# Seven products for both halves of the first FFN, with kept weight parts and an activation that lives in DRAM

## The chip, the cores and the metric

The kernel runs on one core of one Trainium2 chip. The metric is the device time of one execution in microseconds. Beside the times there is one profiled execution, with the span from its first to its last instruction and a trace of every instruction. The engines are PE (TensorE, matrix products), DVE (VectorE), ACT (ScalarE), POOL (GpSimd) and SP (SyncE, which here only issues transfers). ACT and POOL have queues for transfers as well.

## The reference

A bidirectional encoder of two layers is run on 256 prompt tokens and 1024 sample tokens, of width 1024. All arrays are float32. Both layers end in a SwiGLU FFN with inner width 2816:

```python
def _swiglu(h, w_gate, w_up, w_down):
    return (jax.nn.silu(h @ w_gate) * (h @ w_up)) @ w_down

def _trunk(x, ...):
    for i in range(DEPTH):
        j = i // N_MIXERS
        if i % N_MIXERS == 0:
            x = x + _attention(_rms_norm(x, attn_norm_g[j]), w_qkv[j], q_norm_g[j], k_norm_g[j], w_o[j])
        else:
            x = x + _conformer_conv(_rms_norm(x, conv_norm_g[j]), conv_w_in[j], ...)
        x = x + _swiglu(_rms_norm(x, ffn_norm_g[i]), w_gate[i], w_up[i], w_down[i])
    return _rms_norm(x, final_norm_g)
```

The attention ends in `o @ w_o`. The convolution module is a product to twice the width, a gate, a depthwise convolution of width 31 over the tokens, a LayerNorm, a swish and a product back. `_trunk` is applied to the prompt and to the sample.

## The kernel before

**Arithmetic.** Each float32 operand is split into a high part `h` and a low part `l`. ACT casts the high part and DVE subtracts it (`split`, lines 131 and 132). A product is then three matmuls: `wh*h`, `wh*l`, `wl*h`. The 1280 tokens are kept transposed (channels on the 128 partitions, tokens along the free axis) in two halves of 640, `HA` and `HB`. The convolution shifts the cut to 624 and 656 (`CA`, `CB`). A matmul works on half of a half, 320 columns.

**The usual product.** `mm` (line 594) makes one block of 128 output channels from 8 input tiles with 8 x 3 x 2 = 48 matmuls. `weights` (line 138) loads 512 KB of weights to a `raw` buffer and splits them to an `hl` buffer. There are 4 `raw` and 5 `hl` buffers.

**Seven products.** `two_blocks` (line 717) makes two blocks of 128 output channels for both 320-column parts, as a 2 x 2 by 2 x 2 block product with seven block products in place of eight. Each is 4 input tiles x 3 = 12 matmuls (`product`, line 710), so two blocks take 84 matmuls and not 96. `seven` (line 152) loads the two weight blocks to `raw`, forms the sums of their quarters on DVE (lines 170 to 173) and splits the results: three `hl` tiles `t1`, `t3`, `t2` and a half-sized `t4` (tag `h3`, two buffers). `norm7` and `seven_right` (lines 676 and 692) make the activation's sums and splits. The results of the products go to accumulators `y`, `x`, `z` in PSUM, and from there to two rows with copies on ACT and additions on DVE. `acc` hands out four accumulators in turn, to these and to all other products.

**Which FFN uses what.** In layer 0 the first half uses seven products and the second half the usual ones. In layer 1 it is the other way round: first half usual, second half seven. `ffn` takes the blocks of the inner width in groups. With seven products a group is a pair of blocks: gate, then up, then the `down` product of the group before (lines 848 to 854). `down` (line 833) has two weight tiles for a pair; for each of the 8 output tiles it runs 24 matmuls and adds the result on DVE to the tile of `x` that is resident in SBUF (line 840).

**Slots.** Activations of all kinds share 48 slots of 688 columns (`slot`). Three more buffers, tag `ld`, take tiles that come from DRAM (`loaded`). `x_d` in DRAM holds a copy of `x`, by half.

**Order.** The order on PE is written out by hand, by generators that `drive` (line 1107) interleaves: a main generator, and background generators that advance by so many steps at each of its yields. The order on all other queues is made at build time by a planner, which takes each instruction when by its own estimate its inputs and buffers are ready. What runs on the chip is that fixed order; an instruction that is not ready holds up what is queued behind it on its engine. The sequence of layer 0 (lines 1124 to 1143) is: `heads(HA)` splits the attention's output; `attn_out(HA)`, the product with `w_o`, beside `heads(HB)`; `attn_out(HB)`, all 8 output tiles, beside `norm7(HA)`; `ffn(0)` on HA; one group of `ffn(0)` on HB beside the norm of HA; `conv_in` on HA; the rest of `ffn(0)` on HB. The depthwise convolution of HA (`conv_mid`, line 933, 31 DVE instructions for each of 8 tiles) runs as background beside `conv_in` and the rest of that FFN.

Of the kernel before, what the change touches and what calls it, by code (L numbers as in the profile page):

```python
# [69 lines left out]
def trunk(ctx: ExitStack, tc: tile.TileContext, a: dict):  # L70
# [6 lines left out]
    x_d = dram.tile([D, T], F32, name="x_d")  # L77

# [73 lines left out]
    def seven(src1, src2):  # L152


        q = D // 2
        raws = []
        for src in (src1, src2):
            raw = wp.tile([P, D], F32, tag="raw", bufs=RAW, name="raw")
            nc.sync.dma_start(raw.rearrange("p (k c) -> p k c", k=NK), src)
            raws.append(raw)  # L160
        a, b = raws

        def parts(raw):
            hl = wp.tile([P, 2, D], F32R, tag="hl", bufs=WEIGHTS, name="hl")
            split(hl[:, 0, :], hl[:, 1, :], raw)
            return hl

        t1 = parts(a)
        third = hp.tile([P, q], F32, tag="third", bufs=THIRDS, name="third")
        V.tensor_tensor(out=third, in0=a[:, :q], in1=b[:, :q], op=ALU.subtract)  # L170
        V.tensor_tensor(out=b[:, :q], in0=b[:, :q], in1=b[:, q:], op=ALU.add)
        V.tensor_tensor(out=a[:, :q], in0=b[:, :q], in1=a[:, :q], op=ALU.subtract)
        V.tensor_tensor(out=a[:, q:], in0=a[:, q:], in1=a[:, :q], op=ALU.subtract)
        t3, t2 = parts(a), parts(b)
        t4 = hp.tile([P, 2, q], F32R, tag="h3", bufs=THIRDS, name="h3")
        split(t4[:, 0, :], t4[:, 1, :], third)
# [499 lines left out]
    def norm7(half, row, ops, load, box):  # L676
# [4 lines left out]
        for k in range(NK // 2):  # L681
# [7 lines left out]
            seven_right(f[0][:, :n], f[0][:, n:2 * n], f[1], n, ops)  # L689
            yield  # L690

    def seven_right(b11, b12, low, n, ops):

# [10 lines left out]
        for x, pair in ((low, (2, 3)), (t12, (5, 6)), (t34, (7, 4))):  # L704
            h, l = hl_pair("b")
            split(h[:, :2 * n], l[:, :2 * n], x[:, :2 * n])
            for i, c in zip(pair, (slice(0, n), slice(n, 2 * n))):
                ops[i].append((h[:, c], l[:, c]))
# [8 lines left out]
    def two_blocks(src, f, ops, n, corner):  # L717
# [3 lines left out]
        left = seven(*(src[:, g * P:(g + 1) * P].rearrange("(k p) c -> p k c", p=P) for g in (f, f + 1)))  # L721
# [32 lines left out]
    def attn_out(half, os_, xs, each):  # L754
        for ct in range(NK):
# [25 lines left out]
    def ffn(layer, hn, xs, half, groups, closing=None, each=None):  # L781
# [4 lines left out]
        last = groups[-1][-1]  # L786

# [16 lines left out]
        def up2(f):  # L804
# [3 lines left out]
            g1, g2 = two_blocks(a["w_gate"][layer], f, hn, n, gate_corner)  # L808
# [7 lines left out]
            u1, u2 = two_blocks(a["w_up"][layer], f, hn, n, up_corner)  # L816
# [8 lines left out]
        def ups(fs):  # L825
            if isinstance(hn, dict):
                for f in fs[::2]:
                    yield from up2(f)
            else:
                for f in fs:  # L830
                    yield from up(f)

        def down(fs, seen):
            wd = [weights(a["w_down"][layer, f * P:(f + 1) * P, :].unsqueeze(1)) for f in fs]
            acts = [hs.pop(f) for f in fs]
            for ct in range(NK):
                pd = acc("pd")
                o = slice(ct * P, (ct + 1) * P)
                mm(pd, lambda k: (wd[k][:, 0, o], wd[k][:, 1, o]), acts, n, True, True)
                V.tensor_tensor(out=two(xs[ct], half), in0=pd[:, :, :n], in1=two(xs[ct], half), op=ALU.add)  # L840
# [7 lines left out]
        for fs in groups:  # L848
            early = fs if closing is not None and fs[-1] == last else fs[:2 if isinstance(hn, dict) else 1]
            yield from ups(early)  # L850
            if prev is not None:
                yield from down(prev, len(early) == len(fs) and fs[-1] == last)
            yield from ups(fs[len(early):])
            prev = fs
# [22 lines left out]
    def back(xs, half, row, out, box):  # L877

        for ct in range(NK):
            xs.append(slot("x"))  # L880
            nc.sync.dma_start(xs[ct][:, :half.len], x_d[ct * P:(ct + 1) * P, half.lo:half.hi])
        yield from norm(xs, half, row, out, box)

    def sevens():
        return {i: [] for i in range(1, 8)}
# [237 lines left out]
    with tc.manual_schedule(engines={mybir.EngineType.PE}):  # L1123
        oa, ob, xa, xb, ha, hb = [], [], [], [], sevens(), []
# [4 lines left out]
        tot, take = taken(HB)  # L1129
        drive(attn_out(HB, ob, None, take),  # L1130
              first(factors(tot_a, HA, RMS_EPS, box), norm7(HA, R_F0, ha, lambda ct: xa[ct], box)), 2)
        gs = groups(2, 2, 2, 2, 2, 2, 2, 2, 2, 2, 2)
        drive(ffn(0, ha, xa, HA, gs), back(xb, HB, R_F0, hb, box_b), 3, factors(tot, HB, RMS_EPS, box_b))
        hc, u, c, y, box = [], [], [], [], []
        gs = groups(3, 3, 4, 4, 4, 4)
        drive(ffn(0, hb, xb, HB, gs[:1]), norm(xa, HA, R_CONV, hc), 2)
        spill(xa, HA)
        w = CA.len + GAP
        bg = conv_mid(u, w, c, box)
        drive(conv_in(hc, HA, u), bg, RATE0, finish=False)  # L1140
# [57 lines left out]
```

## Time and profile before

| | |
|---|---|
| median of 3 runs | 2964.31 us (2963.46 to 2966.57) |
| profiled execution, its own time | 2959.4 us |
| its span | 2957.4 us |
| mean granted clock of TensorE | 0.991 |
| transfers, read and written | 220.37 MB and 34.01 MB |
| `ffn(0)` on HA | 752.5 to 1194.9 us |
| `ffn(0)` on HB, first group | 1194.9 to 1265.7 us |
| `conv_in` on HA | 1265.7 to 1378.4 us |
| `ffn(0)` on HB, the rest | 1378.4 to 1783.4 us |

The page gives for each engine the time in which it was busy; the view of windows gives the same for a stretch, with the number of instructions begun in it, the granted clock and the busy share of the 16 DMA engines. The timeline lists instructions in order, and in square brackets how long the engine was idle before one and what ended that wait. The chain of waits follows the work that ended last back to its start. The time of the profiled execution lies 4.9 us below the median of the runs.

### The profile page before, as it was taken

Reading aid. Unit: us, or ns where it says so; the run is one execution under the profiler, and the core shown is the slowest. Engines: PE = TensorE matmul, PEld = TensorE weight load, DVE = VectorE, ACT = ScalarE, POOL = GpSimd, SP = SyncE. Lnnn points to the kernel's source line nnn. Section 1 sums busy time; section 2 is a strip of 40 time slices with the busy share of each in tenths; the row PEclk is TensorE's granted clock in tenths of the full one; section 3 lists DMA queues with packets and bytes.
Section 4 is the critical chain, followed back from the end, with each engine's and each line's share of the span. In section 5 each row is a group of like instructions: output and inputs, shape, how many; then the busy total and the mean of one; then the engine's idle time right before and its main releaser. Section 6 shows DMA issues by size and latency. Waiting matters only on the chain.

```text
span 2957.4 us, 46658 instructions
## 1 busy us (share of the span) xinstructions
PE 2876.9 (97%) x18837; PEld 2755.3 (93%) x18837; DVE 2210.3 (75%) x3501; ACT 1179.5 (40%) x1835; POOL 445.4 (15%) x403
## 2 busy tenths in 40 slices
PE   8989999999999999999999999999999998999997
PEld 6767888789999999999999999999999998999997
DVE  7988999965767677677998446889985438767675
ACT  4438888863433333322212234222222324333332
POOL 2545555421100000100000102000001001000000
PEclk9999999999999999999999999999999999999999
DMA  4532232144222223322222224222223322422221
GB/s 151 180 122 58 55 86 60 44 122 124 91 86 82 76 84 121 116 79 74 67 75 68 83 90 139 72 75 76 68 69 94 96 77 94 137 82 73 84 72 51
DMA packets 323680, 262.65 MB, mean 89 GB/s; under 512 B 18392, under 2 KB 285664, under 8 KB 323464
## 3 DMA queue, kind: packets, MB, share of 16 engines
q1 hardware_dynamic: 309688, 240.26, 27.7%
q10 hardware_dynamic: 12336, 14.16, 1.4%
q0 software_dynamic: 1440, 5.24, 0.6%
q8 instruction: 148, 2.42, 0.3%
q14 instruction: 68, 0.56, 0.1%
HBM read 220.37 MB, written 34.01 MB: 86 GB/s over the span
## 4 chain that ended last, share of the span: by engine, by line
PE 52%; DVE 4%; DMA 2%; issue 0%; ACT 0%; DVEq 0%; ACTq 0%
PE pd L603 14%; PE pu L603 10%; PE pg L603 10%; PE ci L916 8%; PE co L603 4%; DVE hl L132 1%; DMA raw<-in_w_up_dram 1%; DMA raw<-in_w_gate_dram 1%; PE y L713 1%; PE y L715 1%; PE y L714 1%; PE z L714 0%; PE z L713 0%; PE z L715 0%; PE pd L1074 0%
## 5 line engine op out<-in xcount | busy, mean ns | idle before, releaser
L131 ACT CAST hl<-raw 128x1024 fp32r<-128x1024 f32 x372 | 385.0, 1048 | 877.5 <-issue 380.9
L132 DVE TENSOR_TENSOR hl<-raw,hl 128x1024 fp32r<-128x1024 f32 x372 | 462.4, 1251 | 157.9 <-ACT hl L131 157.3
L603 PE MATMUL pd<-hh,hl 128*128 128x320 f32 (+2 forms) x2752 | 522.4, 309 | 3.0 <-DVE x L840 3.0
L603 PEld LDWEIGHTS pd<-hh,hl 128*128 128x128 f32 x2752 | 433.2, 188 | 3.9 <-DVE x L840 3.5
L944 DVE SCALAR_TENSOR_TENSOR c<-u,cols,c 128x640 f32<-128x640 f32 (+1 forms) x480 | 427.6, 899 | 9.7
L603 PE MATMUL pd<-hl 128*128 128x320 f32 (+2 forms) x1376 | 313.8, 309 | 1.4 <-DVE hl L132 1.4
L840 DVE TENSOR_TENSOR x<-pd,x 128x640 f32<-128x640 f32 (+2 forms) x264 | 215.3, 822 | 131.8 <-PE pd L603 131.6
L603 PE MATMUL pu<-hnh,hl 128*128 128x320 f32 (+1 forms) x1408 | 269.1, 308 | 0.0
L603 PE MATMUL pg<-hnh,hl 128*128 128x320 f32 (+1 forms) x1408 | 269.0, 308 | 0.0
L632 POOL TENSOR_TENSOR sq<-sq 128x640 f32<-128x640 f32 (+2 forms) x63 | 118.0, 1873 | 958.1 <-ACT sq L628 956.6
L603 PEld LDWEIGHTS pd<-hl 128*128 128x128 f32 x1376 | 230.2, 188 | 2.0 <-DVE hl L132 2.0
L603 PEld LDWEIGHTS pg<-hnh,hl 128*128 128x128 f32 x1408 | 221.5, 189 | 0.0
L603 PEld LDWEIGHTS pu<-hnh,hl 128*128 128x128 f32 x1408 | 220.8, 188 | 0.3
L473 DVE TENSOR_SCALAR_CACHE_REDUCE s<-s,r_q 128x1024 f32<-128x1024 f32 (+1 forms) x160 | 181.0, 1132 | 23.1 <-PE s L461 16.7
L132 DVE TENSOR_TENSOR pl<-pt,ph 128x512 fp32r<-128x512 f32 x272 | 186.8, 687 | 15.2 <-ACT ph L131 10.5
L916 PE MATMUL ci<-hnh,hl 128*128 128x320 f32 (+2 forms) x1024 | 192.6, 309 | 0.0
L495 POOL TENSOR_SCALAR p<-p,rl 128x1024 f32<-128x1024 f32 (+1 forms) x160 | 158.8, 997 | 169.1 <-DVE rl L492 129.2
L502 PEld LDWEIGHTS pt<-ident,p 128*128 128x128 f32 x1088 | 132.2, 141 | 53.0 <-DVE pl L132 17.1
L131 ACT CAST ph<-pt 128x512 fp32r<-128x512 f32 x272 | 159.6, 590 | 48.1 <-PE pt L502 38.5
L502 PE MATMUL pt<-ident,p 128*128 128x128 f32 x1088 | 166.2, 275 | 7.6 <-DVE pl L132 4.3
L916 PEld LDWEIGHTS ci<-hnh,hl 128*128 128x128 f32 x1024 | 164.5, 188 | 0.0
L484 ACT ACTIVATE p<-s,nm 128x1024 f32<-128x1024 f32 (+1 forms) x160 | 159.4, 999 | 10.7 <-DVE s L473 7.5
(230 smaller groups left out, 6129.0 us busy)
## 6 DMA issues: line engine op xcount, KB each, us to landing
raw<-in_w_gate_dram SPq DMA_DIRECT2D x88, 512.0 KB
raw<-in_w_up_dram SPq DMA_DIRECT2D x88, 512.0 KB
raw<-in_w_down_dram SPq DMA_DIRECT2D x88, 512.0 KB
raw<-in_conv_w_in_dram SPq DMA_DIRECT2D x32, 512.0 KB
raw<-in_w_qkv_dram SPq DMA_DIRECT2D x20, 512.0 KB
q_d<-qs SPq DMA_DIRECT2D x18, 512.0 KB
raw<-in_w_o_dram SPq DMA_DIRECT2D x16, 512.0 KB
q<-q_d SPq DMA_DIRECT2D x16, 512.0 KB
```

The costliest lines, as they stand in the source:

```text
L131: S.copy(out=dst_h, in_=src)
L132: V.tensor_tensor(out=dst_l, in0=src, in1=dst_h.bitcast(F32), op=ALU.subtract)
L473: V.tensor_scalar(out=s[:, c], in0=s[:, c], scalar1=r_q[self.j // 4][b][:, i, head:head + 1], scalar2=None, op0=ALU.mult, op1=ALU.min, acc ...
L484: S.activation(out=p[:, c], in_=s[:, c], func=AF.Exp, bias=nm[:, i:i + 1], scale=-1.0, accum_out=l[:, i:i + 1])
L495: GP.tensor_scalar(out=p[:, c], in0=p[:, c], scalar1=rl[:, i:i + 1], scalar2=1.0, op0=ALU.mult, op1=ALU.mult)
L502: PE.transpose(ps[:, n * P:(n + 1) * P], self.p[n][:, kt * P:(kt + 1) * P], ident)
L603: PE.matmul(ps[:, c, :n], wt, x[:, c * n:(c + 1) * n], start=first and k == 0 and not end and xi == 0, stop=last and k == nk - 1 and end)
L632: GP.tensor_tensor(out=self.tot, in0=self.tot, in1=new, op=ALU.add)
L713: PE.matmul(ps, wh, h, start=first and k == 0, stop=False, skip_group_check=True)
L840: V.tensor_tensor(out=two(xs[ct], half), in0=pd[:, :, :n], in1=two(xs[ct], half), op=ALU.add)
L916: PE.matmul(ps[:, c, :hi - lo], wt, x[:, lo:hi], start=k == 0 and not end and xi == 0, stop=k == NK - 1 and end)
L944: V.scalar_tensor_tensor(out=c[:, :ln], in0=us[ct][:, k:k + ln], scalar=col(ct, R_DW + k), in1=c[:, :ln], op0=ALU.mult, op1=ALU.add)
```

## The change

`ffn(0)` on HB now also uses seven products. The first half's `seven` stores each finished part (`t1`, `t3`, `t2`, `t4`, high and low) to a DRAM tensor `w7_d`, 3.67 MB for each matrix and pair of blocks. The second half's `seven` loads these parts straight to `hl` and `h3` and does no splits and no sums for gate and up.

```diff
+    w7_d = {(m, f): dram.tile([P, 7, D], F32, name=f"w7_{m}_{f}") for m in ("w_gate", "w_up") for f in range(0, FF // P, 2)}
...
+        def parts(raw, at_k):
+            n = 2 if at_k < 6 else 1
...
+            flat = hl.rearrange("p h c -> p (h c)").bitcast(F32)
+            if src1 is None:
+                nc.sync.dma_start(flat, keep.rearrange("p n c -> p (n c)")[:, at_k * D:(at_k + n) * D])
+                return hl
             split(hl[:, 0, :], hl[:, 1, :], raw)
+            if keep is not None:
+                nc.sync.dma_start(keep.rearrange("p n c -> p (n c)")[:, at_k * D:(at_k + n) * D], flat)
             return hl
```

The second half's `x` is no longer resident during its FFN. `down` loads each tile from `x_d` to an `ld` buffer, adds in place and stores it back through POOL's queue; in the last group the sum goes to a slot and stays.

```diff
+                if stored:
+                    old = loaded("old")
+                    nc.sync.dma_start(old[:, :ln], x_d[o, half.lo:half.hi])
+                    if fs[-1] == FF // P - 1:
+                        x = slot("x")
+                        xs.append(x)
+                    else:
+                        x = old
+                else:
+                    x = old = xs[ct]
                 mm(pd, lambda k: (wd[k][:, 0, o], wd[k][:, 1, o]), acts, n, True, True)
-                V.tensor_tensor(out=two(xs[ct], half), in0=pd[:, :, :n], in1=two(xs[ct], half), op=ALU.add)
+                V.tensor_tensor(out=two(x, half), in0=pd[:, :, :n], in1=two(old, half), op=ALU.add)
+                if stored and x is old:
+                    nc.gpsimd.dma_start(x_d[o, half.lo:half.hi], x[:, :ln])
```

With seven products a group's order becomes gate, `down` of the group before, up (for both halves of layer 0 and for the second half of layer 1); in the last group both gate and up still come first.

The product with `w_o` for HB is made in two portions: output tiles 0 to 3 before `ffn(0)` on HA, beside `norm7(HA)`, and tiles 4 to 7 after it, beside the norm of HA. The splits of the attention's output for HB are made again for the second portion, beside the end of `ffn(0)` on HA. All of `ffn(0)` on HB now comes after `conv_in`, beside which `norm7(HB)` runs, with tiles of `x` loaded from DRAM; its last two splits of every group of four are put off until `conv_in` has ended.

```diff
+        drive(attn_out(HB, ob, None, take_b, range(NK // 2)),
+              first(factors(tot_a, HA, RMS_EPS, box), norm7(HA, R_F0, ha, lambda ct: xa[ct], box)), 4)
+        ob = []
+        tot_a, take_a = taken(HA)
+        drive(ffn(0, ha, xa, HA, pairs, None, lambda ct: take_a(ct, xa[ct])), heads(HB, ob), 2, iter(()))
+        hc, u, c, y, box, box_a = [], [], [], [], [], []
+        drive(attn_out(HB, ob, None, take_b, range(NK // 2, NK)),
+              first(factors(tot_a, HA, RMS_EPS, box_a), norm(xa, HA, R_CONV, hc, box_a)), 3)
+        xa, later = [], []
...
+        drive(conv_in(hc, HA, u),
+              both(first(factors(tot_b, HB, RMS_EPS, box_b), norm7(HB, R_F0, hb, stored(HB), box_b, later)), bg, RATE0),
+              1, finish=False)
+        for pair, x in later:
+            cut7(hb, HB.n, pair, x)
+        drive(ffn(0, hb, xb, HB, pairs, load=True, stored=True), conv_norm(c, box, w, CA, y), 3, bg, RATE)
```

More of the change, by code (lines that the diff above doesn't have):

```diff
@@ L674, in norm, with norm7 @@
             yield
-    def norm7(half, row, ops, load, box):
+    def norm7(half, row, ops, load, box, later=None):
         n = half.n
@@ L703, in seven_right @@
         V.tensor_tensor(out=t4, in0=b21, in1=t2, op=ALU.subtract)
[L704 to L708, printed above, removed]
+        cut7(ops, n, (2, 3), low)
+        return ((5, 6), t12), ((7, 4), t34)
     def product(ps, left, right, first):
@@ L715, in product, with two_blocks @@
             PE.matmul(ps, wl, h, start=False, stop=k == len(right) - 1, skip_group_check=True)
[L717 to L721 removed]
+    def two_blocks(layer, name, f, ops, n, corner, load):
+        keep = w7_d[name, f] if layer == 0 else None
+        src = a[name][layer]
+        left = seven(*(None if load else src[:, g * P:(g + 1) * P].rearrange("(k p) c -> p k c", p=P)
+                       for g in (f, f + 1)), keep)
         y, x, zz = (acc(name)[:, 0, :n] for name in "yxz")
@@ L752, in heads, with attn_out @@
             yield
-    def attn_out(half, os_, xs, each):
-        for ct in range(NK):
+    def attn_out(half, os_, xs, each, cts=range(NK)):
+        for ct in cts:
             old = loaded("old")
@@ L825, in ups @@
         def ups(fs):
[L826 to L831, printed above, removed]
+            for f in fs:
+                yield from up(f)
         def down(fs, seen):
@@ L848, in ffn @@
         for fs in groups:
[L849 to L853, printed above, removed]
+            ending = fs[-1] == last
+            if paired:
+                g = up2(fs[0])
+                yield next(g)
+                if ending:
+                    yield from g
+                if prev is not None:
+                    yield from down(prev, ending)
+                yield from g
+            else:
+                early = fs if closing is not None and ending else fs[:1]
+                yield from ups(early)
+                if prev is not None:
+                    yield from down(prev, len(early) == len(fs) and ending)
+                yield from ups(fs[len(early):])
             prev = fs
@@ L875, in taken, with stored, load @@
         return tot, take
[L877 to L882, printed above, removed]
+    def stored(half):
+        def load(ct):
+            x = loaded("xb")
+            nc.sync.dma_start(x[:, :half.len], x_d[ct * P:(ct + 1) * P, half.lo:half.hi])
+            return x
+        return load
     def sevens():
```

72 lines of the change are left out of this document (37 added, 35 removed).

## The prediction, made before the changed kernel was run

> **What bounds the kernel now.** I read the page's busy times first, then the chain of waits, then windows cut at the stages that the change touches.
>
> ```profile
> span 2957.4 us, 46658 instructions
> ...
> PE 2876.9 (97%) x18837; PEld 2755.3 (93%) x18837; DVE 2210.3 (75%) x3501; ACT 1179.5 (40%) x1835; POOL 445.4 (15%) x403
> ```
> ```profile
> 1385.42 7.03 PE pu L603 x48
> ```
> ```profile
> 752.50:1194.90 442.40, 434.33 (x2937) 431.83 (x2937) 318.80 (x429) 171.41 (x248) 10.09 (x6) 0.99 0.30 93
> 1194.90:1265.70 70.80, 67.89 (x466) 67.11 (x466) 42.14 (x57) 20.87 (x27) 6.42 (x6) 0.99 0.27 81
> 1265.70:1378.40 112.70, 112.70 (x772) 112.70 (x771) 82.55 (x96) 24.29 (x32) 8.88 (x22) 1.00 0.29 85
> 1378.40:1783.40 405.00, 405.00 (x2774) 404.68 (x2774) 302.56 (x354) 106.30 (x135) 34.62 (x20) 1.00 0.25 76
> ```
> ```profile
> 1045.00:1085.00 40.00, 40.00 (x274) 39.86 (x273) 29.02 (x40) 14.68 (x22) 0.00 (x0) 1.00 0.27 80
> ...
> 1434.00:1512.00 78.00, 78.00 (x535) 78.00 (x534) 76.31 (x91) 16.45 (x19) 4.80 (x2) 1.00 0.25 76
> ```
>
> The columns of a window are its length, then busy time and count for PE, PE's weight loads, DVE, ACT and POOL, then clock, DMA share and GB/s. PE is the bound: 97% of the span, and on the chain a block of 48 matmuls takes 7.03 us, 146.5 ns each. At that rate the 2937 matmuls of the first half's FFN need 430.3 us of its 442.4, so it loses 12.1. The second half's two stretches hold 3240 matmuls, 474.7 of 475.8 us. So in this half a matmul less is time less, as long as nothing else comes to the front. DVE is the next engine: from 1434 to 1512, beside the convolution, it was busy for 76.31 of 78.00 us, and PE still lost nothing.
>
> What PE loses, it loses at the joints between stages:
>
> ```profile
> 698.20 3.57 PE L656 MATMUL bc<-ident,rs_r 80*128 80x80 f32 x16 [3.54 <-DVE rs_r L126]
> ...
> 757.35 0.41 PE L714 MATMUL x<-bl,hl 128*128 128x320 f32 x1 [1.48 <-DVE bl L132]
> ...
> 760.75 0.64 PE L713 MATMUL y<-bh,hl 128*128 128x320 f32 x1 [2.83 <-ACT r L726]
> ```
> ```profile
> 1192.30 0.56 PE L603 MATMUL pd<-hh,hl 128*128 128x320 f32 x2 [2.20 <-DVE x L840]
> ...
> 1204.41 0.56 PE L603 MATMUL pg<-hnl,hl 128*128 128x320 f32 x2 [2.08 <-DVE hnl L132]
> ```
> ```profile
> 764.00:766.00 2.00, 2.00 (x10) 2.00 (x9) 0.34 (x1) 0.43 (x1) 0.00 (x0) 0.50 0.70 205
> ...
> 1194.00:1196.00 2.00, 2.00 (x10) 2.00 (x9) 2.00 (x4) 2.00 (x3) 1.92 (x2) 0.50 0.32 127
> ...
> 1206.00:1208.00 2.00, 2.00 (x15) 2.00 (x15) 1.03 (x1) 0.94 (x2) 0.00 (x0) 1.00 0.58 227
> 752.50:770.00 17.50, 13.18 (x70) 12.66 (x70) 12.45 (x16) 7.36 (x12) 3.22 (x2) 0.80 0.31 99
> ```
>
> The last figure but two of a window is the clock. After the waits of 2.83 and 2.20 us it was 0.50, after 2.08 it stayed at 1.00. The 17.5 us from 752.5 held 70 matmuls, 10.3 us of work: 7.2 were lost, 4.3 of them waiting. So a wait of 2.2 us or more costs some 2 to 3 us beyond itself.
>
> **The change, part by part.**
>
> *Removed.* Gate and up of the second half were 22 x 2 x 48 = 2112 matmuls and become 22 x 84 = 1848. 264 x 146.5 ns = **-38.7 us**. A pair of blocks with its `down` is now 168 + 96 = 264 matmuls, 38.7 us: gate 12.3, `down` 14.1, up 12.3.
>
> *Start of the first FFN.* Before, `norm7` on HA had 8 blocks of the `w_o` product to hide under, now 4. DVE's prices, by the distance between starts:
>
> ```profile
> 737.78 0.49 DVE L700 TENSOR_TENSOR t<-hf 128x320 f32<-128x320 f32 x1
> 738.18 0.49 DVE L702 TENSOR_TENSOR t<-hf 128x320 f32<-128x320 f32 x1
> ```
> ```profile
> 1089.56 1.54 DVE L840 TENSOR_TENSOR x<-pd,x 128x640 f32<-128x640 f32 x2
> ```
> ```profile
> 1103.12 2.36 DVE L132 TENSOR_TENSOR hl<-raw,hl 128x1024 fp32r<-128x1024 f32 x2 [0.49 <-ACT hl L131]
> ```
> ```profile
> 1457.81 7.24 DVE L944 SCALAR_TENSOR_TENSOR c<-u,cols,c 128x640 f32<-128x640 f32 x9
> ```
>
> That is 0.40 for 320 columns, 0.75 for 640, 1.15 for a weight tile, 0.80 for an instruction with three operands. `norm7` takes 4 x (2 x 0.80 + 5 x 0.40 + 3 x 0.75) = 23.4 us; three more `w_o` splits, four additions and the first gate's weights bring some 13. From 701.8, when the factors are spread, DVE ends at 738 at the earliest; PE has three blocks left, 21.1 us, until 722.9. Three of seven products (5.3 us) come after the last operand, so the pass ends at 743 or later, where 735.2 would be unhindered. With the half clock PE loses 10 to 16 us. The old joint lost 7.2. I take **+6** (-3, if the planner packs DVE better, to +14).
>
> *Stores beside the first FFN.* Each pair adds 2 x 3.67 MB to transfers that keep the engines at 0.27.
>
> ```profile
> 1088.00:1089.00 1.00, 1.00 (x9) 1.00 (x9) 1.00 (x2) 0.00 (x0) 0.00 (x0) 1.00 0.74 303
> ...
> 1106.00:1107.00 1.00, 1.00 (x9) 1.00 (x9) 0.00 (x0) 0.00 (x1) 0.00 (x0) 1.00 0.96 271
> ```
> ```profile
> 1168.00:1170.00 2.00, 2.00 (x16) 2.00 (x15) 0.91 (x2) 0.00 (x0) 0.00 (x0) 1.00 1.04 406
> ```
>
> Weights in 512-byte pieces fill the engines at 271 GB/s; rows of 2560 bytes and more reach 406/1.04 = 390, and `w_down`'s 4 KB rows about as much. 7.34 MB at 390 are 18.8 us, with 0.27 x 38.7 = 10.4 that makes 29 of 38.7 us. SP's queue now carries stores that wait for splits, with the next pair's raw loads behind them. With the order gate, `down`, up, the five `hl` buffers come free so that every split has at least 12.3 us (one product pass) before its use, against 6.2 for two raw loads (rows below) and 2.7 for a store ahead of them. What is left is DVE held up by a late raw tile. I take **+4** (0 to +20: the old steady stretch lost nothing, two waits of 1 us in each pair would be 20).
>
> *The joint after the first FFN.* The waits of 2.20 (with its half clock) and 2.08 us go. In their place `factors` and `spread` stand back to back on PE, as at 698.20: 3.54 us and a half clock. **0** (-4 to +6). The second round of splits for HB takes the place of the norm that ran there.
>
> *`conv_in` and the joint after it.* DVE gets 4 x (1.6 + 2.0 + 0.75) = 17.4 us more on 82.55 of 112.7, 89%; less than 98%, which was harmless. The eight late splits, 6.0 us on DVE, need the slots that `conv_in` frees at its end; PE has two products, 3.5 us, before it needs them. **+4** (0 to +12; by my count up to 47 of 48 slots are taken there, and one short means a wait).
>
> *The second FFN.* For each pair DVE has 8 additions (6.0), two splits of `w_down` (2.3), and the seven-product rows and splits (5.4), 13.7 us; six yields with 5 steps of the convolution add 30 x 0.80 = 24.0. 37.7 of 38.7 us, 97%, until the convolution's last 180 steps are through, about six pairs: as before, no slack. The DMA engines carry 7.34 + 1.05 + 2 x 2.62 = 13.6 MB, at 390 GB/s 34.9 us of 38.7, or 90%.
>
> The Trainium skill, DMA: Bandwidth & Descriptors, section Specifications, gives about 358 GB/s as one core's limit to HBM; by that figure, as an estimate, a pair takes 38.1 us and there is no slack at all. The 406 GB/s quoted above lie beyond it, so the trace decides for 390; a cap like that would act through later loads, as the first rival does.
>
> The tile of `x` makes a loop of its own: load, add, store, and only then is the `ld` buffer free.
>
> ```profile
> x<-in_x_sample_dram POOLq DMA_DIRECT2D x8, 512.0 KB, 4.0
> ```
> ```profile
> 1104.37 1.51 SPq L159 DMA_DIRECT2D raw<-in_w_gate_dram  x2
> ```
> ```profile
> 1110.57 0.69 DVE L170 TENSOR_TENSOR third<-raw 128x512 f32<-128x512 f32 x1 [1.00 <-DMA raw<-in_w_gate_dram]
> ```
>
> POOL's 512 KB landed in 4.0 us, so 320 KB in about 3.5. Two raw loads took 6.2 us from issue to use, 3.9 of it data at 271 GB/s, so a load has 2.3 us beside its data, 3.2 us for 320 KB. With the addition and the hand-overs a turn c is 7.7 us, over three buffers 2.6 us for a tile, where PE makes one in 1.76. But four accumulators stand between. The first addition ends 2.75 us after `down` starts, the seventh at 2.75 + 2c = 18.2; the accumulator it frees is first needed by `z` of the up pass at 19.3. It holds with 1.1 us to spare. I take **+12** for all of this (0 to +60): about 2 us in each of six pairs where DVE has no slack.
>
> Sum: -38.7 + 6 + 4 + 0 + 4 + 12 = -12.7, from the execution's own 2959.4 to 2946.7. The runs' median lies 4.9 above that execution: **2951.6**.
>
> **The rivals.**
>
> *Slower: the loop through the three `ld` buffers.* It decides from c = 8.2 us, and every further microsecond costs PE two in each pair, and 2 more once the wait passes 2.2. If the loads of `x` stand behind one kept part on SP's queue (1.05 MB, 2.7 us), c is 10.4, a pair loses 4.4 + 2, ten pairs 64: -38.7 + 14 + 64 = +39, 3004. If the planner gives one buffer away early it is worse:
>
> ```profile
> 1182.82 4.72 SPq L982 DMA_DIRECT2D old<-x_d  x2
> ```
>
> These are `conv_out`'s loads, issued 600 us before its first product: the planner fetches ahead as soon as it can. Two buffers make 3.85 us a tile, some 8 tiles x 2.1 - 5 + 2 = 14 in a pair, 3080. Against it: the margin, and that SP's queue can be ordered to let `x` pass.
>
> The Trainium skill, SBUF — State Buffer, section SBUF: two separate sides, says that a transfer from POOL's queue starves while DVE runs in a two-port mode. No row here shows one beside the convolution; it would lengthen c.
>
> *No change: DVE.* If late tiles of `x` hold DVE up by 3 us a pair, the second FFN loses 18 in six pairs in place of 12, and if late raw tiles cost the first one 14 in place of 4, the sum is +3.3: 2968. For it speaks DVE's 97% in every such pair, against it that the planner puts convolution steps into its gaps.
>
> *Everything hides.* With every added term at 0, -38.7: 2926. For it speaks the row of 1434 to 1512, where DVE at 98% cost PE nothing; against it every joint of the old trace, of which none was free.
>
> That the second half would not use seven products is excluded: its operand is now a dictionary, which is what selects them.
>
> **How the numbers follow.** My forecast (2932 to 2958): 0.48. Everything hides: 0.10. No change: 0.14. Slower: 0.28, of which 0.10 above 3010. So faster 0.58, same 0.14, slower 0.28; 0.2%, 5.9 us, is about what a measurement of this kernel can tell from no change. The range 2932 to 3010 leaves 0.10 out on each side.
>
> **What would show it.** PE must count 18573 matmuls. The first FFN should take some 440 us with its loss in its first 25, `conv_in` 113 to 120, the second FFN 430 to 450 with DVE at 95% or more in its first two thirds. If DVE's addition at the `down` product is what PE waits for, pair after pair, with a load of `x_d` behind it, the first rival is right; if PE waits for kept parts, or the first FFN grows by over 20 us, my reading of the transfers is wrong.

## The result and the profile after

The changed kernel takes **2989.56 us** (median of 4, 2988.44 to 2990.63) beside 2965.44 for the kernel before on the same chip (4 runs, 2963.46 to 2967.71): a ratio of 1.0081, 95% interval 1.0064 to 1.0099. It is slower, where 2951.6 and faster was forecast; the time lies inside the forecast's range of 2932 to 3010, on the other side of no change. The profiled execution took 2990.63 us, its span is 2988.9.

The page of the changed kernel, its span, the busy times and the first line of the chain of waits:

```profile
span 2988.9 us, 47056 instructions
...
PE 2864.2 (96%) x18573; PEld 2733.0 (91%) x18573; DVE 2233.4 (75%) x3606; ACT 1176.0 (39%) x1884; POOL 475.4 (16%) x483
...
PE 71%; DVE 12%; DMA 8%; issue 6%; ACT 2%; POOL 1%; DVEq 0%; SPq 0%; ACTq 0%; POOLq 0%
```

The 264 matmuls are gone: 18573. In a kernel with fewer matmuls the span has grown by 31.5 us, so PE idles or runs at half rate some 70 us more. On the page of the kernel before the chain could be followed for 58% of the span: PE 52%, DVE 4%, transfers 2%. Here 8% are transfers and 12% DVE. Windows, cut at the stages, tell where (columns as in the prediction). First the changed kernel: the product with `w_o` (first portion), the first FFN's first 50 us and its rest, the second portion of `w_o`, `conv_in`, the second FFN, then everything up to layer 1's last FFN, and that to the end.

```profile
685.00:722.60 37.60, 34.08 (x224) 34.02 (x223) 29.79 (x51) 14.58 (x21) 5.07 (x3) 0.91 0.63 195
722.60:772.90 50.30, 41.89 (x255) 40.40 (x255) 38.21 (x55) 23.93 (x36) 6.25 (x1) 0.90 0.72 244
772.90:1162.40 389.50, 389.50 (x2653) 389.14 (x2652) 280.81 (x368) 147.82 (x214) 5.48 (x4) 1.00 0.80 272
1162.40:1204.30 41.90, 34.65 (x227) 34.33 (x226) 24.29 (x34) 13.57 (x17) 11.17 (x9) 0.88 0.42 129
1204.30:1323.20 118.90, 117.14 (x801) 116.88 (x800) 95.97 (x139) 26.18 (x38) 6.16 (x23) 0.99 0.39 119
1323.20:1804.10 480.90, 444.44 (x2942) 434.61 (x2941) 340.22 (x465) 116.35 (x195) 68.28 (x97) 0.99 0.84 299
1804.10:2410.70 606.60, 606.60 (x4223) 606.25 (x4222) 453.37 (x540) 163.85 (x199) 62.10 (x48) 1.00 0.30 89
2410.70:2988.90 578.20, 543.98 (x3621) 537.03 (x3620) 390.33 (x614) 199.04 (x296) 12.92 (x8) 0.98 0.28 82
```

And the kernel before, the stages that the prediction did not show: the product with `w_o`, the same long stretch, and the last stage.

```profile
687.00:752.50 65.50, 61.96 (x414) 61.90 (x413) 44.94 (x73) 22.57 (x33) 17.64 (x6) 0.95 0.40 114
...
1783.40:2388.70 605.30, 605.30 (x4222) 604.96 (x4220) 455.06 (x541) 164.50 (x200) 56.10 (x45) 1.00 0.30 86
2388.70:2957.40 568.70, 539.64 (x3621) 534.19 (x3619) 387.18 (x614) 198.62 (x296) 12.89 (x8) 0.99 0.28 84
```

Length less count x 146.5 ns is what a stage loses. How that loss changed, stage by stage:

| stage | lost before | lost after | change | forecast |
|---|---|---|---|---|
| `w_o` for HB, one portion or two | 4.8 | 4.8 + 8.6 | +8.6 | |
| first FFN after its start, with its end | 4.9 | 0.8 | -4.1 | |
| first group of the second FFN, now gone | 2.5 | 0 | -2.5 | |
| *these three, the joints and the stores* | | | *+2.0* | 0 and +4 |
| first FFN, its start | 7.2 | 12.9 | +5.7 | +6 |
| `conv_in` | -0.4 | 1.6 | +2.0 | +4 |
| second FFN | -1.4 | 49.9 | **+51.3** | +12 |
| up to layer 1's last FFN | -13.2 | -12.1 | +1.1 | 0 |
| last stage | 38.2 | 47.7 | **+9.5** | 0 |

The sum is +71.6; with -38.7 for the matmuls that is +33, and the stretch before `w_o` is 2 us shorter: 31, beside 31.5 by the spans. (The half microsecond is in matmuls on the border of two windows, which both count. A negative loss means that some of a stage's matmuls take less than 146.5 ns; that cancels in the difference.) Two rows hold nearly all that the forecast lacks: the second FFN, 39 us more than forecast, and the last stage, 9.5.

What PE waits for most in the second FFN, by the view of waits for that stretch (engine, line, waited for: us in total, times, longest):

```profile
PE pd L613 <- DVE old L871: 11.9, 12, 2.5
PE z L733 <- DVE r L751: 8.4, 5, 1.8
PE x L733 <- DVE old L871: 4.5, 1, 4.5
PE pd L613 <- DVE x L871: 3.8, 4, 1.9
```

Line 871 is the addition of a `down` product to the tile of `x` in an `ld` buffer. PE waits for an accumulator that this addition, or one of the rows queued behind it, has yet to empty. All waits of the view add up to 36.5 us, and for 13.7 us, in three stretches, the granted clock stood at 0.50, which is another 6. Why the addition is late stands in the timeline of DVE, POOL and SP, beside the convolution:

```profile
1409.39 0.82 DVE L871 TENSOR_TENSOR old<-pd,old 128x640 f32<-128x640 f32 x1
...
1418.89 0.82 DVE L871 TENSOR_TENSOR old<-pd,old 128x640 f32<-128x640 f32 x1 [2.44 <-DMA old<-x_d]
...
1430.49 0.82 DVE L871 TENSOR_TENSOR old<-pd,old 128x640 f32<-128x640 f32 x1 [1.14 <-DMA old<-x_d]
```
```profile
1410.62 0.54 POOL L873 DMA_DIRECT2D x_d<-old  x1 [20.41 <-DVE old L871]
...
1420.12 0.55 POOL L873 DMA_DIRECT2D x_d<-old  x1 [5.91 <-DMA old<-x_d]
```
```profile
1415.93 1.82 SPq L862 DMA_DIRECT2D old<-x_d  x3
1420.94 0.32 SPq L167 DMA_DIRECT2D hl<-w_w_gate  x1
1423.04 6.27 SPq L862 DMA_DIRECT2D old<-x_d  x2
```

These are one buffer's turns in a pair: addition at 1409.39, store at 1410.62, next load at 1415.93, next addition at 1418.89, 9.5 us later; then store at 1420.12, load at 1423.04 behind a kept part (`w_w_gate`, 1 MB) issued at 1420.94, and the addition 7.45 us after its issue, a turn of 11.6. DVE stands idle at the end of both and waits for the transfer. The additions of the nine pairs from 1366 to 1730 show 18 such turns, 179.8 us in all, a mean of **10.0 us**. The forecast had worked with 7.7 and with 8.2 as the point from which it costs.

By its legs the mean turn is 1.5 us from the addition to the store's issue, 4.0 from there to the next load's issue and 4.5 from that to the next addition. The two turns of a pair are long in different legs, as the one shown is. In the first five pairs the first turn has 4.7 to 6.0 us from store to load and 3.0 from load to addition; the second has 2.6 to 3.3 and, behind a kept part issued just before, 6.2 to 7.5.

Where no convolution is left, the same is seen with DVE mostly idle:

```profile
1670.84 0.82 DVE L871 TENSOR_TENSOR old<-pd,old 128x640 f32<-128x640 f32 x1 [3.02 <-PE pd L613]
...
1681.54 0.83 DVE L871 TENSOR_TENSOR old<-pd,old 128x640 f32<-128x640 f32 x1 [6.40 <-DMA old<-x_d]
```
```profile
1672.07 0.54 POOL L873 DMA_DIRECT2D x_d<-old  x1 [22.19 <-DMA hl<-w_w_up]
```
```profile
1678.08 7.52 SPq L862 DMA_DIRECT2D old<-x_d  x4
```

Addition at 1670.84, store at 1672.07, the load of the same buffer at 1678.08, 6.0 us after the store, and the next addition at 1681.54. The view of transfers for 1323 to 1763 gives the store's time from issue to landing, at an engine share of 0.84 over the stage:

```profile
x_d<-old POOLq DMA_DIRECT2D x72, 320.0 KB, 5.1
```

### The profile page after: what moved, and what is told of

It is laid out like the page before. It is cut to its first block, busy times and chain, and to the rows that moved or that the text cites. A ratio compares the mean times of both kernels' runs of the same rounds, so it can differ in the third digit from the quotient of the medians.

```text
span 2988.9 us, 47056 instructions
## 1 busy us (share of the span) xinstructions
PE 2864.2 (96%) x18573; PEld 2733.0 (91%) x18573; DVE 2233.4 (75%) x3606; ACT 1176.0 (39%) x1884; POOL 475.4 (16%) x483
## 4 chain that ended last, share of the span: by engine, by line
PE 71%; DVE 12%; DMA 8%; issue 6%; ACT 2%; POOL 1%; DVEq 0%; SPq 0%; ACTq 0%; POOLq 0%
PE pd L613 14%; PE ci L961 5%; PE pg L613 5%; PE pu L613 5%; PE s L471 4%; PE pt L512 4%; PE co L613 4%; PE y L733 4%; PE y L735 4%; PE y L734 4%; PE wo L613 3%; DMA old<-x_d 3%; DVE c L989 3%; DMA x_d<-old 2%; PE o L524 2%
## 5 line engine op out<-in xcount | busy, mean ns | idle before, releaser
L132 ACT CAST hl<-raw 128x1024 fp32r<-128x1024 f32 x328 | 340.1, 1048 | 729.2 <-PE pd L613 304.7
L613 PE MATMUL pd<-hh,hl 128*128 128x320 f32 (+2 forms) x2752 | 528.9, 311 | 15.8 <-DVE old L871 11.9
L133 DVE TENSOR_TENSOR hl<-raw,hl 128x1024 fp32r<-128x1024 f32 x328 | 406.2, 1247 | 126.7 <-ACT hl L132 126.0
L613 PEld LDWEIGHTS pd<-hh,hl 128*128 128x128 f32 x2752 | 434.9, 189 | 21.1 <-DVE old L871 12.5
L871 DVE TENSOR_TENSOR x<-pd,x 128x640 f32<-128x640 f32 (+2 forms) x216 | 177.6, 825 | 127.4 <-PE pd L613 126.4
L733 PE MATMUL y<-bh,hl 128*128 128x320 f32 (+1 forms) x528 | 168.0, 318 | 24.0 <-DVE r L757 11.7
L733 PE MATMUL z<-bh,hl 128*128 128x320 f32 (+1 forms) x528 | 165.3, 313 | 10.2 <-DVE r L751 8.4
L735 PE MATMUL y<-bh,hl 128*128 128x320 f32 (+1 forms) x528 | 165.5, 313 | 0.3 <-DVE hl L133 0.3
L734 PE MATMUL y<-bl,hl 128*128 128x320 f32 (+1 forms) x528 | 165.7, 314 | 0.0
L734 PE MATMUL z<-bl,hl 128*128 128x320 f32 (+1 forms) x528 | 164.6, 312 | 0.0
```

The source lines that it names most:

```text
L132: S.copy(out=dst_h, in_=src)
L133: V.tensor_tensor(out=dst_l, in0=src, in1=dst_h.bitcast(F32), op=ALU.subtract)
L613: PE.matmul(ps[:, c, :n], wt, x[:, c * n:(c + 1) * n], start=first and k == 0 and not end and xi == 0, stop=last and k == nk - 1 and end)
L733: PE.matmul(ps, wh, h, start=first and k == 0, stop=False, skip_group_check=True)
L734: PE.matmul(ps, wh, l, start=False, stop=False, skip_group_check=True)
L735: PE.matmul(ps, wl, h, start=False, stop=k == len(right) - 1, skip_group_check=True)
```

## The experiments

The theory after reading: the second FFN is slow by the loop load, addition, store through three `ld` buffers, and the last FFN by its new order. The rivals: DVE, which has 97% of work beside the convolution; the transfers, at 0.84 to 0.9 of their engines; and for the joints the second broadcast product.

**Without the loop.** The second half's FFN loads one tile of `x` once; the other loads and all stores of `x` are left out, the additions stay (their sums are then not the reference's).

```diff
-                    old = loaded("old")
-                    nc.sync.dma_start(old[:, :ln], x_d[o, half.lo:half.hi])
+                    if not once:
+                        once.append(loaded("old"))
+                        nc.sync.dma_start(once[0][:, :ln], x_d[o, half.lo:half.hi])
+                    old = once[0]
...
-                if stored and x is old:
-                    nc.gpsimd.dma_start(x_d[o, half.lo:half.hi], x[:, :ln])
```

> Leaves out the loads and stores of x in the second half's first FFN, but for one load: the eight additions of each pair go to one tile that stays in an ld buffer, so the sums are not the reference's. DVE has the same number of additions. Theory A (the loop load-add-store through three ld buffers holds PE up): the FFN falls from 480.9 to about 435-440 us, the kernel to 2943-2950. Theory B (DVE, 97% loaded beside the convolution): the FFN stays above 465, the kernel above 2975. Theory C (the kept parts arrive late because the transfer engines are full): in between, about 2955-2970, since a third of the bytes goes.

Measured: 2952.87 us, 0.9971 of before (0.9960 to 0.9983). The second FFN takes 442.4 us in place of 480.9: **the loop costs 38.5**. The stage lies 2.4 us above theory A's range, the kernel's time between the ranges of A and C. By itself the run does not part the loop from the transfers, whose share of their engines falls from 0.84 to 0.59 with it; the next two runs do. What stays is 11.4 over the 431.0 of its matmuls: some 7 beside the convolution, and 4.5 in the first 40 us, where PE waits 2.9 us for a copy on ACT. Windows of 160 us beside the convolution, this kernel and then the changed one:

```profile
1403.00:1563.00 160.00, 156.60 (x1057) 154.57 (x1056) 158.50 (x209) 29.82 (x52) 6.26 (x4) 1.00 0.60 211
```
```profile
1403.00:1563.00 160.00, 148.25 (x979) 144.65 (x978) 147.53 (x194) 24.98 (x45) 23.42 (x36) 0.99 0.89 319
```

Without the loop DVE is at 99% and PE loses 160 - 1057 x 0.1465 = 5.1 us. With it PE loses 16.6, and DVE has 12.5 us of idle time, 8.2 of them in wait for tiles of `x`. So DVE is not the limit in the changed kernel; it would be the next one.

A window of 160 us cuts pairs differently from kernel to kernel, so where the loop costs its time is better read from pair to pair, between the starts of the `down` products in PE's timeline. The last two `down` products stand back to back, with no gate or up between them.

| us | six pairs, most of them beside the convolution | seventh | eighth and ninth | last two `down` |
|---|---|---|---|---|
| changed kernel, three buffers | 256.7 | 48.9 | 94.6 | 40.6 |
| no loop | 240.1 | 40.2 | 91.2 | 29.3 |
| parts kept once (next run) | 246.8 | 49.3 | 92.2 | 39.5 |
| four buffers (below) | 259.8 | 43.5 | 91.5 | 33.1 |
| five buffers (best kernel, below) | 243.5 | 41.2 | 92.3 | 30.1 |

The loop costs 2.8 us in each of the six pairs, 8.7 in the seventh and 11.3 in the last two `down` products. Three kernels with the same loop (the changed one, the old order and the later norm, below) differ by 3.6 us in the first column, so less than that means nothing there.

**The kept parts once.** The transfers are emptied without touching the loop: the parts of `w_gate` and `w_up` are loaded for the first matrix only and used again for all (the products are then not the reference's).

```diff
-            t1, t3, t2, t4 = (parts(None, k) for k in (0, 2, 4, 6))
+            if not held:
+                held.extend(parts(None, k) for k in (0, 2, 4, 6))
+            t1, t3, t2, t4 = held
```

> Leaves out the second half's loads of kept parts after the first: one set of t1, t3, t2, t4 is loaded and used for all 22 matrices of pairs, so the products are not the reference's. The loop of x stays as it is. Theory A with contention (the loop is long because the transfer engines are busy): a turn falls from 10.7 to under 8.2 us, the FFN to 435-445, the kernel to 2945-2955. Theory A without contention (the loop is long by its own latencies): the FFN stays at 470-480, the kernel above 2975. Theory B: no change. Theory C: FFN 435, kernel 2945.

Measured: 2985.27 us, 1.0082 (1.0069 to 1.0095); the second FFN takes 470.5 us, as theory A without contention has it.

```profile
1403.00:1563.00 160.00, 153.42 (x1021) 150.89 (x1019) 151.21 (x202) 28.56 (x50) 25.51 (x36) 0.99 0.47 158
```

The engines' share falls from 0.89 to 0.47, and in the six pairs the turn falls from 9.9 us to 7.8: 2.5 to 4.5 from store to load and 3.0 to 3.7 from load to addition. So both long legs were long because of the kept parts' transfers. But the stage wins only 10.4 of the 38.5 us: the six pairs win 9.9 of the 16.6 that the loop costs there, the seventh pair nothing. Even at 7.8 us DVE still waits 7.5 us for tiles of `x` in these 160, so a threshold of 8.2 looks too kind. How much too kind is not shown: the run has a cost of its own, since three of the five `hl` buffers are held for good.

**Five `ld` buffers.** Two of the 48 slots are given for them; everything is computed.

```diff
-SLOTS, SQUARES, LOADS = 48, 3, 3
+SLOTS, SQUARES, LOADS = 46, 3, 5
```

> Five ld buffers in place of three, 46 slots in place of 48; all is computed. Theory A: a tile of x then costs 10.7/5 = 2.1 us in place of 3.6, the accumulators cover the rest: the FFN falls to 435-450, the kernel to 2945-2960, unless two slots fewer cost something at the joints (up to 10). Theories B and C: 2985-2995.

Measured: 2957.51 us, 0.9986 (0.9978 to 0.9995). The second FFN takes 448.2 us, 32.7 less than with three, and both times lie in theory A's ranges, though the transfers are as many as before and faster. The timeline of a kernel with five buffers and two more edits (below) shows why:

```profile
1403.27 0.82 DVE L871 TENSOR_TENSOR old<-pd,old 128x640 f32<-128x640 f32 x1
...
1407.85 0.82 DVE L871 TENSOR_TENSOR old<-pd,old 128x640 f32<-128x640 f32 x1
1410.17 0.83 DVE L871 TENSOR_TENSOR old<-pd,old 128x640 f32<-128x640 f32 x1
1412.93 0.82 DVE L871 TENSOR_TENSOR old<-pd,old 128x640 f32<-128x640 f32 x1 [1.15 <-DMA old<-x_d]
```

Five additions of a pair now follow each other at the products' pace, with no wait; the sixth comes 9.66 us after the first. The turn is no shorter (a mean of 9.9 in nine pairs of this kernel), but only three of eight additions wait for one. This window of the same kernel, at an engine share of 0.92, loses 6.5 us:

```profile
1399.00:1559.00 160.00, 155.19 (x1048) 153.37 (x1047) 156.28 (x205) 29.31 (x51) 23.50 (x36) 1.00 0.92 339
```

So the rival that the transfers themselves are full falls too: they carry 339 GB/s here against 319 in the slower kernel.

**The old order in layer 1.** Gate, up, `down` for layer 1's last FFN, as before the change.

```diff
-                if ending:
+                if ending or layer == 1:
```

> Layer 1's last FFN gets its old order back: gate, up, then down of the pair before. Theory: the new order is what made that stage 9.5 us longer (PE waits there for the addition to c22), so 2978-2982. Rival: the stage is longer for another reason (its place in time, other noise of the schedule): 2987-2992.

Measured: 2983.16 us, 1.0075 (1.0060 to 1.0090). Its last stage, and what PE waits for most often there, first in the changed kernel, then in this one:

```profile
PE y L733 <- DVE r L757: 9.1, 9, 2.3
```
```profile
2411.00:2980.90 569.90, 540.88 (x3623) 535.55 (x3621) 387.54 (x614) 198.88 (x296) 12.92 (x8) 0.98 0.28 84
```
```profile
PE y L733 <- DVE r L757: 5.1, 7, 1.5
```

569.9 us in place of 578.2; before it was 568.7. The kernel's time alone does not show it: it lies 1 us above the theory's range, single runs go from 2976 to 2990, and the two ratios' intervals overlap. But the stage does, in all kernels that were profiled: from the first seven-product matmul of layer 1's last FFN to the end of the span, the six with the new order took 489.4 to 497.3 us, the eight with the old order 481.0 to 484.7.

**The store through ScalarE's queue.**

```diff
-                    nc.gpsimd.dma_start(x_d[o, half.lo:half.hi], x[:, :ln])
+                    nc.scalar.dma_start(x_d[o, half.lo:half.hi], x[:, :ln])
```

> The x of layer 1's first FFN goes back to x_d through ScalarE's DMA queue instead of GpSimd's; everything else as in the changed kernel (2989.6). Theory A (in the turn add, store, load of one ld buffer, the 5 to 6 us between the store's issue and the next load's issue are partly the path of GpSimd's queue): the turn falls from 9.2-11.6 to under 9 us, this FFN from 480.9 to 455-470 us, the kernel 2965 to 2980. Theory B (the 5 to 6 us are the transfer's own, on engines that are 84% busy, so the queue does not matter; ScalarE's instruction stream adds waits of its own): turn within 1 us of before, 2985 to 2995.

Measured: 2989.54 us, 1.0104 (1.0089 to 1.0120). Neither theory as written. The turns of the five pairs beside the convolution fall from 10.1 to a mean of 8.0 us, as A said; the kernel's time does not fall, as B said. The second FFN does get shorter, 471.1 us in place of 480.9 in the profiled execution, whose 2984.34 us are the lowest of four; that is just outside A's 455 to 470, and it does not show in the median. Nor is it the store's path that A had in mind: from store to load the turns win half a microsecond, and most of the gain is in the load's leg of the second turns, 4.0 to 4.4 us in place of 6.2 to 7.5. Part of what holds the gain back can be read in the timeline of ACT:

```profile
1427.81 0.33 ACTq L873 DMA_DIRECT2D x_d<-old  x1
1428.17 0.42 ACT L753 COPY r<-y 128x320 f32<-128x320 f32 x1 [3.66 <-DVE old L871]
1432.40 0.33 ACTq L873 DMA_DIRECT2D x_d<-old  x1
1432.77 0.43 ACT L755 COPY r<-z 128x320 f32<-128x320 f32 x1 [4.17 <-DVE old L871]
```

Each store waits on ACT for DVE's addition, and the copies that empty the accumulators of the up product stand behind it; PE then waits for `r` of line 755 (7 times, 9.4 us in the second FFN). That wait is not among those of the changed kernel: a part of the waiting has moved from one queue to another. All of PE's waits in the stage add up to 30 us, against 36.5. (The window from 1403 to 1563 holds 1000 matmuls, against 979, but also 999 in the next kernel, which leaves the store where it was.)

**The second broadcast product.** In the second portion of `w_o` the norm's steps are held back by two behind the factors (`pause(2)` only yields twice).

```diff
-              first(factors(tot_a, HA, RMS_EPS, box_a), norm(xa, HA, R_CONV, hc, box_a)), 3)
+              first(factors(tot_a, HA, RMS_EPS, box_a), pause(2), norm(xa, HA, R_CONV, hc, box_a)), 3)
```

> In the second portion of w_o behind layer 1's conv-less first half, the steps that norm HA are held back by two steps behind the factors, so that the broadcast product meets its operand already written; nothing else is changed against the changed kernel (2989.6). Theory A (the two portions cost 14 us more than one because the second broadcast product waits 6.3 us for DVE's row of factors and TensorE then runs some 3 us at half rate): attn_out's second portion falls from 41.9 to 33-36 us, the kernel to 2981-2984. Theory B (the later norm is then missing at the head of conv_in, which takes up the gain): 2987-2992, with conv_in longer than 118.9 us by the same amount.

Measured: 2986.26 us, 1.0091 (1.0077 to 1.0105). The broadcast product in the timeline of PE, in the changed kernel and in this one, and then this one's windows of the portion and of `conv_in`:

```profile
1178.19 3.67 PE L666 MATMUL bc<-ident,rs_r 80*128 80x80 f32 x16 [6.33 <-DVE rs_r L127]
```
```profile
1182.09 1.91 PE L666 MATMUL bc<-ident,rs_r 80*128 80x80 f32 x16
```
```profile
1165.80:1197.90 32.10, 31.23 (x225) 30.96 (x225) 21.23 (x31) 12.64 (x16) 11.35 (x7) 1.00 0.57 170
1197.90:1320.00 122.10, 119.38 (x802) 118.25 (x801) 98.95 (x141) 27.19 (x40) 6.27 (x25) 0.97 0.38 115
```

The wait is gone, the 16 products take half the time, and the portion takes 32.1 us in place of 41.9, at a clock of 1.00 and not 0.88. But the norm's parts are then late in `conv_in`: by the start of the second FFN's `down`, about half of it has been given back. In the kernel's time what is left cannot be told from nothing: 1.0091 beside 1.0081, and 2986.26 us lies between the ranges of the two theories.

**Together: five buffers, old order, later norm.**

> Five ld buffers (46 weight slots in place of 48), layer 1's last FFN in its old order gate, up, down, and the norm of the second portion of w_o two steps later, on top of the change. Theory A (the losses are three separate places: loop 32 us, order 8.5 us, broadcast 6-8 us): they add up, 2957.5 - 6.4 - 7 = 2941 to 2946, faster than the kernel before by 0.5 to 0.7%. Theory B (with the loop mended the engine that is bound in the second FFN, DVE at 97-99%, or the transfers at over 90%, takes the rest back): 2951 to 2957, about the same as five buffers alone.

Measured: **2944.48 us** (5 runs, 2942.42 to 2947.73), 0.9952 (0.9939 to 0.9964): faster than the kernel before by 16 us on the same chip and, by the two ratios, than the changed one by some 38, with everything computed. Theory A holds, with the time in its range: the three losses are separate places, and what their ends win adds up. Its span is 2940.6 us with the same 18573 matmuls.

**Around that kernel.** Six buffers with 45 slots; four with 47; five with 45 slots; the norm held back by one step; and the first portion's norm held back by three steps.

> As best5 but six ld buffers and 45 weight slots. Theory A (the loop of x through five buffers still binds in places of the second FFN, which took 448.2 us with five buffers and 442.4 without the loop): 3 to 6 us less than best5. Theory B (what is left is DVE's 97-99% and the transfers' 92-99%; more buffers change nothing, a weight slot less costs up to a few us): within 2 us of best5 or slower by up to 6.

> As best5 (2944.5) with four ld buffers and 47 weight slots. Theory A (the loop of x binds by the number of buffers: eight additions of a pair of down products in a period of 41 us at a turn of 9 to 11 us; three buffers need 2.67 turns, four need 2, which is 18 to 22 us beside the 16 us of the products): the second FFN takes 452 to 462 us, between 481 with three and 448 with five, the kernel 2948 to 2960. Theory B (one buffer more is enough, the rest of five's gain was the additions' position): 2942 to 2946.

> As best5 (2944.5) with 45 weight slots in place of 46. It tells what cost best6 its 11 us in conv_in behind the second FFN, where TensorE waited 10.8 us at one place for ScalarE. Theory A (the 45 slots: another slot order of the weights shifts the cuts): that wait of about 10 us comes back and the kernel takes 2953 to 2957. Theory B (the sixth ld buffer, by the later time at which x leaves it): no such wait, 2943 to 2947.

> As best5 (2944.5) with the norm HA of the second portion of w_o held back by one step in place of two. Theory A (at two steps the broadcast's wait falls by 9.8 us and conv_in's first products lose 4.7 us to norms that come late; at one step the broadcast is still early and the norms are there): 2940 to 2943. Theory B (one step is not enough for the broadcast, or what conv_in loses does not depend on it): 2944 to 2952.

> As best5 (2944.5), with the steps norm HA of the first portion of w_o also held back, by three steps, behind the factors. Theory A (the first broadcast product's wait of 3.5 us and the half rate behind it, which the kernel before has too, go in the same way): the first FFN begins 3 to 6 us earlier, 2938 to 2942. Theory B (seven-product operands of the first FFN come later by as much, since DVE is what it waits for in its first 25 us): 2944 to 2950.

| | median us | ratio, 95% | second FFN, from its first `down` product |
|---|---|---|---|
| changed kernel, three buffers | 2989.56 | 1.0081 (1.0064 to 1.0099) | 440.8 |
| four, 47 slots | 2961.55 | 1.0001 (0.9993 to 1.0010) | 428.0 |
| five, 46 slots | 2944.48 | 0.9952 (0.9939 to 0.9964) | 407.0 |
| five, 45 slots | 2963.29 | 1.0006 (0.9997 to 1.0014) | 407.0 |
| six, 45 slots | 2955.53 | 0.9984 (0.9975 to 0.9993) | 402.6 |
| five, one step | 2956.49 | 0.9982 (0.9974 to 0.9990) | 405.5 |
| five, first portion too | 2945.57 | 0.9945 (0.9933 to 0.9957) | 410.2 |
| no loop (parts left out, above) | 2952.87 | 0.9971 (0.9960 to 0.9983) | 400.8 |

(The first and the last row have neither the old order nor the later norm. The rows were measured on several chips; each ratio is to the kernel before on the same one.) The last column falls with the number of buffers: 441, 428, 407, 403, and 401 where there is no loop. Four buffers lie between three and five, as theory A has it, but its sizes miss: I had expected well over half of the way, and it is 38%. And by the table of pairs that part is won in the seventh pair and the last two `down` products alone; in the six pairs four buffers take 259.8 us, no less than three. PE's largest wait with four is for the rows of line 757, 16.7 us in 6 waits over the stage, where the changed kernel has 2.6; why is not taken apart.

Six buffers lost in another place more than they won: 2955.53 us is slower than both theories allowed. PE waits once in the next `conv_in`, and the kernel with five buffers and the same 45 slots has the wait too, by the view of waits of each:

```profile
PE ci L965 <- ACT sg L973: 10.8, 1, 10.8
```
```profile
PE ci L965 <- ACT sg L973: 10.5, 1, 10.5
```

So this wait comes with the slot, not with the sixth buffer, as theory A of the slots said; the time is 6 us above A's range. The rest of the 19 us between 46 and 45 slots is not explained: runs of that kernel differ by 14 us among themselves, and its profiled one, 2953.95 us, is its fastest.

One step is not enough, theory B: the broadcast product still waits 5.2 us and the portion takes 40.9 us in place of 32.0. The time is 4 us above B's range. The first portion's wait of 3.5 us goes with three steps and the first FFN starts 6.5 us earlier. Its wait for the first operand is then longer (6.5 us in place of 5.1), so its first `down` product comes 4.7 us earlier, and the second portion, 1.5 us longer, and the second FFN, 3 us longer, take that back: 2945.57, no better. Theory A missed there.

## Why the prediction was wrong

**The matmuls, -38.7: right.** 18573, and every later stage with the same count as before runs at its old rate or has a cause of its own.

**The start of the first FFN, +6: right, by its mechanism too.** 12.9 us lost in place of 7.2. DVE's last split of the operand began at 738.3, where 738 had been reckoned as its end at the earliest, and the first pass of seven products ended at 747.

**The stores beside the first FFN, +4: 0.** The stretch from 772.9 on lost 0.8 us in 389.5, at 272 GB/s and an engine share of 0.80. Splits, stores and raw loads on one queue cost PE under 1 us.

**The joints, 0: +2**, inside their range. The old two, 4.0 and 2.5 us with the FFN's end, went; the second broadcast product brought 8.6, a wait of 6.33 and not 3.54 among it.

**`conv_in`, +4: +2**, inside its range, but by luck: it was priced for late splits and short slots, and PE's only wait there is 1.8 us for the sums of squares on POOL, with 3.4 us at half clock behind it.

**The second FFN, +12: +51.3. This is the step that failed**, and in it the price of one turn of the `ld` loop, c = 7.7. The mechanism and its place were set out as the first rival; I put the chance of it at 0.28 by a margin of half a microsecond in c. The runs give 10.0 for c. Of the legs, the store's was 3.5 in the forecast and is 4.0, the load's was 3.2 and is 4.5, and the addition with the hand-overs was 1.0 and is 1.5. Behind the means stand 5 us for the store in the first turn of a pair and 6 to 7 for the load in the second, the load behind a kept part that the rival names: its c = 10.4 for that case was close, the second turns of the first five pairs take 10.4 to 11.6. The 3.5 came from POOL loads of 512 KB that landed in a median of 4.0 us. The old trace could have warned of it: of those loads in the first 60 us, the four that took 3.7 to 4.6 us flew at an engine share of 0.44 to 0.66, and the one at 13.56 us, at a share of 1.02, took 6.94. The second FFN's engines stand at 0.84 to 0.9.

The rival's price does not come out. At c = 10.0 it says 2 x 1.8 us in a pair, and 2 more for the half clock once the wait passes 2.2, so 56 in ten pairs; the runs show 38.5. Without the half clock it would be 36, and that this lies near is luck: the six pairs pay 2.8 each, not 3.6, the seventh 8.7, and the last two `down` products, which the rival did not set apart, 11.3. Nor is 2.2 us a limit for the clock. The changed kernel's clock falls to 0.50 for 3.4 us after a wait of 2.08 us (until 736.82) and one of 1.76 (until 1514.83), and stays at 1.00 after one of 2.90 (until 1329.80) and six others of 1.56 to 1.87 in the second FFN. The rival's example of 10.4 gave 3004 for the kernel, the measurement is 2989.6. What the forecast counted as DVE, about 12 us in six pairs, has the right size: 11.4 remain in the stage without the loop, some 7 of them beside the convolution.

The Trainium skill, SBUF — State Buffer, section SBUF: two separate sides, was weighed there as something that would lengthen c through DVE's two-port modes. The trace does not bear that out as the cause: a gap of 6.0 us from store to load stands at 1367.60, beside the convolution, and another at 1672.07, where DVE was busy for 29.37 of the 80 us from 1643; and with the parts kept once the gaps fall to 2.5 to 4.5 us, on the same queue and beside the same convolution.

**The order, not priced.** The prediction tells of gate, `down`, up as a help for the `hl` buffers and gives it no cost in layer 1. So this term stood at nothing without a reason. It costs 8.3 us there by the run with the old order, of the 9.5. What in the order costs it was not taken apart; PE's waits for the rows of line 757 fall from 9.1 to 5.1 us with the old one. The change says that the order holds for layer 1's second half too, and I priced layer 0 alone.

**The rivals.** The first was right in its mechanism, not in its price. "No change by DVE" is excluded as the cause, since DVE was idle for 12.5 of 160 us, 8.2 of them waiting for tiles of `x`. "Everything hides", at 2926, was off by 64 us.

**What remains** in the best kernel, 16.8 us of span gained out of 38.7, are, by the same count, mainly the first FFN's start and some 17 us in the second FFN; the run without the loop keeps 11 of those, so the loop still takes about 6.

## What to carry to other kernels

Where resident data is moved to DRAM, the price is a loop: work out the turn from the slowest leg under the load that the change itself makes, not from a transfer of an idle stage, and compare turn over buffers with the pace of the consumer; if the margin is smaller than the error of one leg, the slower case is the likelier one. The cure was enough more buffers, five here and not four, and not another queue: moving the store to another engine's queue put a part of the wait before that engine's instructions. Where the consumer's turns follow each other with no other work between, as at the last two `down` products, reckon the loop apart. And price a new order for every place that shares the code, also where the reason for it does not hold.

## What the runs showed of the hardware

A store of 320 KB took a median of 5.1 us from issue to landing at an engine share of 0.84 for the stage. Loads of 512 KB at the start of the kernel before took 3.7 to 4.6 us at shares of 0.44 to 0.66, and one took 6.94 at 1.02. Loads and stores together moved 339 GB/s over 160 us at a share of 0.92. The 16 small broadcast products took 3.67 us behind a wait of 6.33 us and 1.91 us with none before them, and the granted clock of that portion was 0.88 in the one kernel and 1.00 in the other. In the changed kernel the clock fell to 0.50 for 3.4 us after waits of PE of 2.08 and 1.76 us, and did not after one of 2.90 and six of 1.56 to 1.87. In the kernel without the loop it did fall after the same wait of 2.90 (until 1330.46). So here the length of a wait alone does not tell.
